# The second token tile's last products held behind the first tile's, a tail of three blocks in two streams, and a shorter log1p

## The chip, the cores and the metric

The kernel runs on one core of a Trainium2 chip. The metric is the device time of one execution in microseconds (us), the median of the runs shown. The core's engines are called PE (TensorE matmul), DVE (VectorE), ACT (ScalarE), POOL (GpSimd) and SP (SyncE, which issues the transfers).

## The reference

The program is two chained transformers of two layers each, on 256 tokens of width 1024, in fp32. Cut to what the change touches:

```python
def first_block(x, p, ...):                     # two layers
    for layer in range(2):
        hn = rmsnorm(h, gains[0])
        mix = mixer_ab(hn, ...) if layer % 2 == 0 else mixer_c(hn, ...)
        h = h + rmsnorm(mix, gains[1])
        hn = rmsnorm(h, gains[2])
        ff = square(relu(hn @ w_up[layer])) @ w_down[layer]
        h = h + rmsnorm(ff, gains[3])
        gate = sigmoid(h @ w_ple_gate[layer])
        h = h + gate * (p[layer] @ w_ple[layer])
def second_block(x, mem, ...):                  # two layers
    for l in range(2):
        h = rms_norm(x) @ w_in[l]               # columns of five attention groups
        o_a, o_b, o_c, o_d = mla(h), fox(h), moba(h), diff(h)
        o_e = memory_attention(h, rms_norm(mem) @ mem_w_kv[l])
        x = x + concat(o_a, o_b, o_c, o_d, o_e) @ w_o[l]
        xn = rms_norm(x)
        x = x + (silu(causal_conv(xn @ w_gate)) * (xn @ w_up)) @ w_down
```

`mixer_ab` (gated delta rule and mLSTM) turns its gate inputs with softplus and log-sigmoid, and fox (attention with a forget gate) does so with a log-sigmoid; both are built on log(1 + e) with e = exp(-|y|).

## The kernel before

**Tiling.** The 256 tokens are two token tiles, t = 0 and t = 1, of 128 rows. The residual `h` lies with tokens on partitions; its transposed halves `aTh` and `aTl` are the operands of the products. Each fp32 product is done as three products of split operands (`hi`/`lo` of the weight with `aTh`/`aTl` or with `w` tiles), which `nmm` (L806) writes. A product of 128 rows with 512 columns adds into a PSUM bank (`ps`).

**Streams.** `stream` (L819) runs such products over weight blocks: `seq` gives pairs (block, tile), and `nmm` is called for each. `lagged(n, lag)` lets tile 1 follow tile 0 by `lag` blocks; `tail_lagged(n, tail)` alternates the tiles, but in the last `tail` blocks writes all of tile 0's first and then tile 1's. When a tile's last block is written, `done` spawns that tile's further chain (bias, norm, transposes, next stage). Streams with one column block (one pair of banks for each tile) are the output projections `w0o`, `w1o` and `wo{l}`, the gate `wg{l}`, the memory projection `wk{l}` and the narrow `wi0{l}`; `wd{l}`, the down projection of `ff1` (L1526), is written by its own loop and has four banks in `down`.

**What sets the order.** The code issues nothing directly. `Recorder.note` (L341) records every operation with a cost (`price`, L365), its predecessors (who wrote or read its tiles before) and a lag to each engine (`LAG`, L265). `order` then lists them again: of the operations that are ready, each engine gets the one that can start first, and among those the one with the highest rank, which is the longest path of costs and lags to the end of the program. The best of seven such arrangements is issued by `issue`, so that every instruction of the profile bears the line L613 (L625 in the changed kernel), and groups are told apart by tile names. Weights come over SP's queue into 2 `raw` buffers, ACT and DVE split them into 4 `hi`/`lo` buffers, there are 32 `w2` buffers, and 8 PSUM banks.

**Where stages meet.** After `wd{l}`'s last product for a tile, `post(t)` does: a multiplication on DVE, two squares with row sums on ACT, the reciprocal root on POOL, a scaled addition into `h` on DVE, and then transposes of `h` on PE (eight of 128x128 for a tile), copies to `aTh`/`aTl`, and the products of `wg{l}`. Each other meeting of two stages has such a chain too.

Of the kernel before, what the change touches and what calls it, by code (L numbers as in the profile page):

```python
# [15 lines left out]
OP = mybir.AluOpType  # L16
# [241 lines left out]
class Recorder:  # L258
# [7 lines left out]
           "act": {"pe": 271, "act": 160, "dve": 142, "pool": 155, "sp": 1220},  # L266
           "dve": {"pe": 270, "act": 128, "dve": 127, "pool": 155, "sp": 1220},
           "pool": {"pe": 200, "act": 90, "dve": 69, "pool": 97, "sp": 1220},
           "sp": dict.fromkeys(("pe", "act", "dve", "pool", "sp"), 2050)}

    def __init__(self, nc):
        self.engines = {"pe": nc.tensor, "act": nc.scalar, "dve": nc.vector, "pool": nc.gpsimd, "sp": nc.sync}
        self.ops, self.pools, self.tile_pool, self.seen = [], {}, {}, {}
        self.run = None


    @contextmanager
    def together(self, share=1):

        self.run = []  # L280
        yield
        op = self.ops[self.run[0]]
        op.cost = op.cost / share + 200 * (share > 1)
        self.run = None

    def engine(self, name):
        rec = self
# [53 lines left out]
    def note(self, eng, call, args, kwargs):  # L341
        op = Op()
        op.eng, op.call, op.args, op.kwargs = eng, call, args, kwargs
        op.preds, op.succs, op.tiles, op.alt, op.more = {}, [], [], None, []
        op.table = self.TABLES.get(args[2], 0) if call == "activation" and args[2] != AF.Copy else None
        isap = lambda x: hasattr(x, "tensor") or hasattr(x, "tag_meta")
        outs = [kwargs[k] for k in ("out", "accum_out") if k in kwargs and isap(kwargs[k])]
        ins = [v for k, v in kwargs.items() if k not in ("out", "accum_out") and isap(v)]
        rest = [a for a in args if isap(a)]
        if "out" not in kwargs:  # L350
            outs.append(rest.pop(0))
        op.cost, op.lag = self.price(op, outs[-1], rest + ins), self.LAG[eng]
        if self.run:
            i = self.run[0]
            first = self.ops[i]
            first.more.append((call, args, kwargs))
            first.cost += op.cost
            op = first
        else:
            i = len(self.ops)  # L360
            self.ops.append(op)
            if self.run is not None:
                self.run.append(i)
        for x, write in [(x, False) for x in rest + ins] + [(x, True) for x in outs]:
            for b in self.boxes(x):  # L365
                self.touch(i, op, b, write)
# [294 lines left out]
def program(ctx, tc, A, out, dbg=None):  # L661
    nc = tc.nc
    rec = Recorder(nc)
    act, dve, pe, sp, pool = (rec.engine(n) for n in ("act", "dve", "pe", "sp", "pool"))
# [150 lines left out]
    def tail_lagged(n, tail):  # L815
        s = [(i, t) for i in range(n - tail) for t in range(2)]
        return s + [(i, t) for t in range(2) for i in range(n - tail, n)]

    def stream(name, items, acts, kpb, halves_, n, seq, done, before=None):  # L819


        first, last = {}, {}
        for t in range(2):
            for i, tt in seq:
                if tt == t:
                    first.setdefault((items[i][0], t), i)
                    last[items[i][0], t] = i
        banks, live = {}, {}
        w = halves_ * n
        for i, t in seq:  # L830
            c, b, k0 = items[i]
            if i not in live:
                live[i] = block(name, b, kpb, w)
            if before is not None:
                before(items[i], t)
            if (c, t) not in banks:
                banks[c, t] = [acc() for _ in range(halves_)]
            hi, lo = live[i]
            for j in range(kpb):
                nmm(banks[c, t], acts(t, k0 + j), hi[:, j, :], lo[:, j, :],  # L840
                    first[c, t] == i and j == 0, last[c, t] == i and j == kpb - 1, n)
                if (j + 1) * 3 * halves_ % 6 == 0:
                    loom.step()
            if last[c, t] == i:
                done(c, t, banks.pop((c, t)))

    def a_T(t, k):
# [251 lines left out]
    def mixer_ab(end):  # L1099
        nab = gain(14)  # L1100
        done = {}
        st = {}

        def gates(bank):
# [4 lines left out]
            e, u, z, ln = (w2()[:, :256] for _ in range(4))  # L1109
# [1 line left out]
            act.activation(e, e, AF.Exp)  # L1111
            dve.tensor_scalar(u, e, 1.0, None, op0=OP.add)
            act.activation(ln, u, AF.Ln)
            dve.tensor_scalar(u, u, -1.0, None, op0=OP.add)
            dve.scalar_tensor_tensor(z, u, 0.0, e, op0=OP.is_equal, op1=OP.mult)
            dve.tensor_scalar(u, u, 1e-30, None, op0=OP.max)
            dve.reciprocal(u, u)
            dve.tensor_tensor(ln, ln, e, op=OP.mult)
            dve.tensor_tensor(ln, ln, u, op=OP.mult)
            dve.tensor_tensor(ln, ln, z, op=OP.add)  # L1120
            dve.scalar_tensor_tensor(ln, y, 0.0, ln, op0=OP.max, op1=OP.add)
            ca = small(1)
            act.activation(ca, col("alog"), AF.Exp)
# [314 lines left out]
            loom.join(*([("B", j - 2)] if j >= 2 else [("A", j, t)]))  # L1438

        items = [(0, j, 2 * j) for j in (2, 3, 0, 1)]  # L1440
        stream("w0o", items, lambda t, k: done[k // 2, t](k % 2), 2, 2, 512, tail_lagged(4, 2), end, before)


    def mixer_c(r, end):
# [32 lines left out]
        def nat_done(c, t, banks):  # L1477
# [2 lines left out]
        items = [(c, 2 * c + i, 4 * i) for c in (2, 0, 1) for i in range(2)]  # L1480
        stream("w1n", items, a_T, 4, 1, 512, lagged(6, 2), nat_done)
        items = [(0, j, 2 * j) for j in range(4)]
        stream("w1o", items, lambda t, k: done[k // 2, t](k % 2), 2, 2, 512, tail_lagged(4, 2), end,
               lambda it, t: loom.join(("C", it[1], t)))


# [209 lines left out]
    def mixers2(l, r, e, mem, tab, lam, end):  # L1696
# [70 lines left out]
        def forget():  # L1767

            y, e, u, z, ln, lg = (small(8) for _ in range(6))
            for t in range(2):  # L1770
                dve.tensor_copy(y[:, 4 * t : 4 * t + 4], st["fx", t])
            dve.scalar_tensor_tensor(e, y, -1.0, y, op0=OP.mult, op1=OP.min)
            act.activation(e, e, AF.Exp)
            dve.tensor_scalar(u, e, 1.0, None, op0=OP.add)
            act.activation(ln, u, AF.Ln)
            dve.tensor_scalar(u, u, -1.0, None, op0=OP.add)
            dve.scalar_tensor_tensor(z, u, 0.0, e, op0=OP.is_equal, op1=OP.mult)
            dve.tensor_scalar(u, u, 1e-30, None, op0=OP.max)
            dve.reciprocal(u, u)
            dve.tensor_tensor(ln, ln, e, op=OP.mult)  # L1780
            dve.tensor_tensor(ln, ln, u, op=OP.mult)
            dve.tensor_tensor(ln, ln, z, op=OP.add)
            dve.scalar_tensor_tensor(lg, y, 0.0, ln, op0=OP.min, op1=OP.subtract)
            yield
            yield
            b = wk()
            pe.matmul(b[:, 0:4], cfv("triu"), lg[:, 0:4], start=True, stop=True)
            pe.matmul(b[:, 4:8], cfv("triu"), lg[:, 4:8], start=True, stop=False)
            pe.matmul(b[:, 4:8], cfv("ones"), lg[:, 0:4], start=False, stop=True)
            c = small(8)  # L1790
            dve.tensor_scalar(c, b[:, 0:8], -8.0, None, op0=OP.mult)
            st["decay"] = c
# [368 lines left out]
```

## Time and profile before

| what | value |
|---|---|
| device time, median of 3 runs | 1399.25 us (1395.28 to 1400.75) |
| the profiled execution's own time | 1395.2 us |
| its span in the trace | 1393.4 us |
| PE busy | 1359.3 us (98%) |
| DVE busy | 998.3 us (72%) |
| ACT busy | 786.4 us (56%) |
| POOL busy | 56.4 us (4%) |

The span is what lies between the first and the last instruction of the trace; the profiled execution's own time is 1.8 us longer, and 4.05 us below the median of the runs. Busy shares are averages over the whole program, whose stages have different limits. Of PE's row, ends of pipelined products are modelled, so idle time inside a dense run of products does not all show.

### The profile page before, as it was taken

To read this page: it belongs to the slowest core of one execution; us is meant where nothing else is said; L and a number is where in the kernel's file an instruction comes from. 1 tells how busy PE (TensorE), PEld (TensorE's weight loads), DVE (VectorE), ACT (ScalarE), POOL (GpSimd) and SP (SyncE) were. 2 spreads that over 40 slices of the span, in tenths; PEclk is the share of its full clock that TensorE was granted. 3 is DMA by queue.
4 is the path that set the end of the run, shared out by engine and by line. 5 is a ranking of instruction groups with operands and counts; after the bars stand their busy time and mean duration, and the time that the engine had idled before them with its cause. 6 is when DMAs were issued, how large, how long until landed. Compare 5 with 4: busy or idle time off the path is not lost.

```text
span 1393.4 us, 23108 instructions
## 1 busy us (share of the span) xinstructions
PE 1359.3 (98%) x8768; PEld 1199.4 (86%) x8774; DVE 998.3 (72%) x2417; ACT 786.4 (56%) x1800; POOL 56.4 (4%) x93
## 2 busy tenths in 40 slices
PE   6999999999999999999999999999999999999998
PEld 6899889999787799998787877999998877899997
DVE  6994876666677876566789798575767999576664
ACT  6665554444554854445576596454546679364443
POOL 0000210000010010000020000000001000000000
PEclk9999999999999999999999999999999999999999
DMA  8332354445543364445555243454545523345553
GB/s 329 134 126 99 114 212 182 182 184 194 212 147 141 139 224 179 185 182 194 207 193 206 91 142 132 152 211 153 212 155 205 187 90 99 144 153 210 182 189 114
DMA packets 36400, 236.36 MB, mean 170 GB/s; under 512 B 4160, under 2 KB 4416, under 8 KB 10176
## 3 DMA queue, kind: packets, MB, share of 16 engines
q1 hardware_dynamic: 36288, 234.88, 46.4%
q8 instruction: 69, 1.13, 0.3%
q14 instruction: 43, 0.35, 0.1%
HBM read 233.82 MB, written 1.05 MB: 169 GB/s over the span
## 4 chain that ended last, share of the span: by engine, by line
PE 88%; DVE 6%; ACT 4%; issue 1%; DMA 1%; SPq 0%; POOLq 0%; POOL 0%; ACTq 0%; DVEq 0%
PE ps L613 88%; ACT w L613 3%; DVE w L613 3%; DVE s L613 2%; DMA cf<-in_cf 1%; DVE lo L613 1%; ACT hi L613 1%; DVE h L613 0%; ACT L613 0%; SPq L613 0%; POOLq L2157 0%; DVE hi L613 0%; ACT aTh L613 0%; POOL s L613 0%; ACTq L613 0%
## 5 line engine op out<-in xcount | busy, mean ns | idle before, releaser
L613 ACT ACTIVATE hi<-raw 128x512 fp32r<-128x512 f32 (+1 forms) x793 | 437.6, 620 | 297.7 <-PE ps L613 244.9
L613 DVE TENSOR_TENSOR lo<-raw,hi 128x512 fp32r<-128x512 f32 (+1 forms) x844 | 526.0, 678 | 51.4 <-ACT hi L613 48.1
L613 PE MATMUL ps<-hi,w 128*128 128x512 f32 (+1 forms) x1272 | 379.1, 395 | 0.5 <-ACT w L613 0.5
L613 PE MATMUL ps<-aTl,hi 128*128 128x256 f32 x1256 | 316.7, 280 | 0.0
L613 PE MATMUL ps<-aTh,hi 128*128 128x256 f32 x1256 | 316.3, 281 | 0.0
L613 PE MATMUL ps<-aTh,lo 128*128 128x256 f32 x1256 | 312.5, 280 | 0.0
L613 PEld LDWEIGHTS ps<-hi,w 128*128 128x128 f32 x1272 | 225.2, 188 | 36.1 <-issue 1.9
L613 PEld LDWEIGHTS ps<-aTh,hi 128*128 128x128 f32 x1256 | 224.8, 188 | 9.4 <-ACT hi L613 0.4
L613 PEld LDWEIGHTS ps<-aTl,hi 128*128 128x128 f32 x1256 | 225.1, 188 | 8.3 <-issue 0.4
L613 PEld LDWEIGHTS ps<-aTh,lo 128*128 128x128 f32 x1256 | 223.6, 189 | 9.9 <-DVE lo L613 1.0
L613 PE MATMUL ps<-lo,w 128*128 128x512 f32 (+1 forms) x636 | 205.9, 393 | 0.0
L613 ACT ACTIVATE w<-ps 128x512 f32<-128x512 f32 (+3 forms) x261 | 128.3, 535 | 130.4 <-PE ps L613 119.9
L613 PE MATMUL ps<-hi,aTh 128*128 128x512 f32 (+2 forms) x480 | 148.4, 366 | 3.7 <-ACT w L613 2.5
L613 DVE CAST hi<-raw 128x512 fp32r<-128x512 f32 x51 | 21.8, 427 | 177.8 <-PE ps L613 177.8
L613 PE MATMUL ps<-lo,aTh 128*128 128x512 f32 (+2 forms) x480 | 147.2, 365 | 0.0
L613 PE MATMUL ps<-hi,aTl 128*128 128x512 f32 (+2 forms) x480 | 147.2, 365 | 0.0
L613 ACT ACTIVATE w<-w 128x512 fp32r<-128x512 f32 (+5 forms) x143 | 74.9, 535 | 95.3 <-DVE w L613 93.0
L613 PEld LDWEIGHTS ps<-lo,w 128*128 128x128 f32 x636 | 112.6, 188 | 17.0 <-issue 0.8
L613 PE MATMUL ps<-cf,w 128*128 128x128 f32 (+1 forms) x572 | 94.7, 279 | 17.4 <-DMA cf<-in_cf 10.6
L613 PE MATMUL ps<-w,w 128*64 128x128 f32 (+10 forms) x912 | 109.5, 299 | 0.6 <-ACT w L613 0.5
L613 PEld LDWEIGHTS ps<-w,w 128*128 128x128 f32 (+4 forms) x912 | 88.7, 171 | 20.0 <-ACT w L613 7.4
L613 PEld LDWEIGHTS ps<-hi,aTh 128*128 128x128 f32 x480 | 86.8, 190 | 16.2 <-ACT w L613 2.8
(105 smaller groups left out, 1143.8 us busy)
## 6 DMA issues: line engine op xcount, KB each, us to landing
raw<-in_wu SPq DMA_DIRECT2D x32, 1024.0 KB, 4.8
raw<-in_wd SPq DMA_DIRECT2D x32, 1024.0 KB, 5.0
raw<-in_fg SPq DMA_DIRECT2D x22, 1024.0 KB, 4.8
raw<-in_fu SPq DMA_DIRECT2D x22, 1024.0 KB, 4.8
raw<-in_fd SPq DMA_DIRECT2D x22, 1024.0 KB, 4.8
raw<-in_wi SPq DMA_DIRECT2D x20, 1024.0 KB, 4.8
raw<-in_w0t SPq DMA_DIRECT2D x10, 1024.0 KB, 5.5
raw<-in_wo SPq DMA_DIRECT2D x10, 1024.0 KB, 4.8
```

The source lines that it names most:

```text
L613: getattr(self.engines[op.eng], call)(*args, **kwargs)
```

## The change

There are four parts. A context `behind` gives every PE operation recorded in it a further predecessor. `stream` uses it in streams with one column block: once tile 0's last block is written, the last recorded operation is kept in `ended`, and all products of tile 1 that are written afterwards may start only behind it. `tail_lagged` gets 3 in place of 2 in `w0o` and `w1o`. In the table of lags SP to SP goes from 2050 to 0. And log1p is done with four operations in place of seven, in `gates` (tiles of 128x256) and `forget` (8 wide).

```diff
-           "sp": dict.fromkeys(("pe", "act", "dve", "pool", "sp"), 2050)}
+           "sp": {"pe": 2050, "act": 2050, "dve": 2050, "pool": 2050, "sp": 0}}
...
+    @contextmanager
+    def behind(self, *ops, only=None):
+        self.hold, self.only = ops, only
+        yield
+        self.hold = ()
+
+    def last(self):
+        return len(self.ops) - 1
...
             self.ops.append(op)
+            if self.hold and self.only in (None, eng):
+                op.preds.update(dict.fromkeys(self.hold, True))
...
-                nmm(banks[c, t], acts(t, k0 + j), hi[:, j, :], lo[:, j, :],
-                    first[c, t] == i and j == 0, last[c, t] == i and j == kpb - 1, n)
+                with rec.behind(*(ended if t else ()), only="pe"):
+                    nmm(banks[c, t], acts(t, k0 + j), hi[:, j, :], lo[:, j, :],
+                        first[c, t] == i and j == 0, last[c, t] == i and j == kpb - 1, n)
                 if (j + 1) * 3 * halves_ % 6 == 0:
                     loom.step()
             if last[c, t] == i:
+                if t == 0 and len(last) == 2:
+                    ended.append(rec.last())
                 done(c, t, banks.pop((c, t)))
...
             act.activation(ln, u, AF.Ln)
-            dve.tensor_scalar(u, u, -1.0, None, op0=OP.add)
-            dve.scalar_tensor_tensor(z, u, 0.0, e, op0=OP.is_equal, op1=OP.mult)
-            dve.tensor_scalar(u, u, 1e-30, None, op0=OP.max)
-            dve.reciprocal(u, u)
-            dve.tensor_tensor(ln, ln, e, op=OP.mult)
-            dve.tensor_tensor(ln, ln, u, op=OP.mult)
-            dve.tensor_tensor(ln, ln, z, op=OP.add)
+            dve.scalar_tensor_tensor(u, u, -1.0, e, op0=OP.add, op1=OP.subtract)
+            dve.tensor_scalar(z, e, 0.5, -1.0, op0=OP.mult, op1=OP.add)
+            dve.tensor_tensor(u, u, z, op=OP.mult)
+            dve.tensor_tensor(ln, ln, u, op=OP.add)
...
-        stream("w0o", items, lambda t, k: done[k // 2, t](k % 2), 2, 2, 512, tail_lagged(4, 2), end, before)
+        stream("w0o", items, lambda t, k: done[k // 2, t](k % 2), 2, 2, 512, tail_lagged(4, 3), end, before)
...
-        stream("w1o", items, lambda t, k: done[k // 2, t](k % 2), 2, 2, 512, tail_lagged(4, 2), end,
+        stream("w1o", items, lambda t, k: done[k // 2, t](k % 2), 2, 2, 512, tail_lagged(4, 3), end,
```

PE has the same products and transposes in both kernels; their order differs. Two places follow, each on PE.

**The end of `wd0` and the start of `wg0`.** Here ps_537 and ps_538 are the banks of tile 0's down projection, ps_539 and ps_540 those of tile 1; ps_735 and ps_736 take the transposes of h_81 (tile 0), ps_744 and ps_745 those of h_82 (tile 1); ps_749 and ps_750 are `wg0`'s banks of tile 0, ps_757 one of tile 1. Before:

```order
L613 MATMUL ps_539<-hi_725,w_720 128x512
L613 MATMUL ps_537<-hi_725,w_719 128x512
L613 MATMUL ps_538<-hi_725,w_719 128x512
L613 MATMUL ps_537<-lo_726,w_719 128x512
L613 MATMUL ps_537<-hi_725,w_720 128x512
L613 MATMUL ps_538<-lo_726,w_719 128x512
L613 MATMUL ps_538<-hi_725,w_720 128x512
L613 MATMUL ps_744<-cf,h_82 128x128 x4
L613 MATMUL ps_745<-cf,h_82 128x128 x4
L613 MATMUL ps_735<-cf,h_81 128x128 x4
L613 MATMUL ps_757<-hi_747,aTh 128x512
```

All four down banks end together, and the transposes of both tiles follow with nothing between them. In the changed kernel tile 0's banks end earlier:

```order
L625 MATMUL ps_538<-hi_725,w_720 128x512
L625 MATMUL ps_537<-hi_725,w_720 128x512
L625 MATMUL ps_539<-hi_711,w_697 128x512
L625 MATMUL ps_540<-hi_711,w_697 128x512
L625 MATMUL ps_539<-lo_712,w_697 128x512
L625 MATMUL ps_540<-lo_712,w_697 128x512
```

Between this and the next piece stand 27 more products of tile 1's banks; they end so:

```order
L625 MATMUL ps_540<-hi_725,w_719 128x512
L625 MATMUL ps_735<-cf,h_81 128x128 x4
L625 MATMUL ps_539<-lo_726,w_719 128x512
L625 MATMUL ps_540<-lo_726,w_719 128x512
L625 MATMUL ps_539<-hi_725,w_720 128x512
L625 MATMUL ps_540<-hi_725,w_720 128x512
L625 MATMUL ps_736<-cf,h_81 128x128 x4
L625 MATMUL ps_750<-hi_747,aTh 128x512
L625 MATMUL ps_750<-lo_748,aTh 128x512
```

After 12 more products of `wg0` for tile 0, tile 1's transposes begin, one at a time among further products of tile 0:

```order
L625 MATMUL ps_750<-lo_753,aTh 128x512
L625 MATMUL ps_749<-lo_748,aTh 128x512
L625 MATMUL ps_744<-cf,h_82 128x128
L625 MATMUL ps_750<-hi_752,aTl 128x512
L625 MATMUL ps_744<-cf,h_82 128x128
```

Tile 0's down products have moved ahead of tile 1's, and tile 1's transposes behind tile 0's gate products. The end of `wd1` and the start of `wg1` have moved in the same way; there 21 products stand between the last of `wd1` and the first transpose of tile 1.

**The end of `w0o`.** ps_476 and ps_477 are tile 0's two banks, ps_478 and ps_479 tile 1's; ps_529 and ps_533 belong to `wp0`, whose products need nothing of `w0o`; ps_500, ps_501, ps_516 and ps_517 take the transposes that follow. Before:

```order
L613 MATMUL ps_476<-lo_488,w_367 128x512
L613 MATMUL ps_476<-hi_487,w_367 128x512
L613 MATMUL ps_478<-hi_487,w_386 128x512
L613 MATMUL ps_477<-lo_488,w_367 128x512
L613 MATMUL ps_477<-hi_487,w_367 128x512
L613 MATMUL ps_478<-lo_488,w_386 128x512
L613 MATMUL ps_478<-hi_487,w_386 128x512
L613 MATMUL ps_479<-hi_487,w_386 128x512 x2
L613 MATMUL ps_479<-lo_488,w_386 128x512
L613 MATMUL ps_479<-hi_487,w_386 128x512
L613 MATMUL ps_533<-hi_527,w_524 128x512
```

Tile 0's banks end 9 and 6 products ahead of the last product of `w0o`. Eighteen products of `wp0` lie between the last of `w0o` and the first transposes (of ps_500). In the changed kernel one bank of tile 0 ends some 55 products ahead of the other banks,

```order
L625 MATMUL ps_478<-lo_475,w_438 128x512
L625 MATMUL ps_479<-lo_475,w_438 128x512
L625 MATMUL ps_476<-hi_474,w_431 128x512
L625 MATMUL ps_477<-hi_487,w_367 128x512
L625 MATMUL ps_478<-hi_474,w_438 128x512
L625 MATMUL ps_479<-hi_474,w_438 128x512
```

and the other ends with tile 1's:

```order
L625 MATMUL ps_476<-hi_487,w_367 128x512
L625 MATMUL ps_478<-hi_487,w_386 128x512
L625 MATMUL ps_476<-lo_488,w_367 128x512
L625 MATMUL ps_476<-hi_487,w_367 128x512
L625 MATMUL ps_479<-hi_487,w_386 128x512
L625 MATMUL ps_478<-lo_488,w_386 128x512
L625 MATMUL ps_478<-hi_487,w_386 128x512
L625 MATMUL ps_479<-lo_488,w_386 128x512
L625 MATMUL ps_479<-hi_487,w_386 128x512
L625 MATMUL ps_529<-hi_527,w_524 128x512
```

The predecessor that `behind` adds is the last operation of ps_477, the second bank in the order written; ps_476's products are not held to it and have moved to the end. There are 22 products of `wp0` now between the last of `w0o` and the first transposes.

## Rows read from the trace of the kernel before

**Rows 1.** The page: busy time by engine; the chain that ended last.

```profile
PE 1359.3 (98%) x8768; PEld 1199.4 (86%) x8774; DVE 998.3 (72%) x2417; ACT 786.4 (56%) x1800; POOL 56.4 (4%) x93
...
PE 88%; DVE 6%; ACT 4%; issue 1%; DMA 1%; SPq 0%; POOLq 0%; POOL 0%; ACTq 0%; DVEq 0%
```

**Rows 2.** Waits of PE over the span: for what, us in total, times, longest.

```profile
PE ps L613 <- ACT w L613: 6.6, 13, 2.5
PE ps L613 <- DVE w L613: 3.9, 3, 1.8
```

**Rows 3.** Timeline, 375 to 381 us: start, length, engine, what, [idle before <-releaser].

```profile
375.50 0.69 DVE L613 TENSOR_TENSOR w<-ps,gb 128x512 f32<-128x512 f32 x1 [1.30 <-PE ps L613]
...
378.49 0.56 POOL L613 TENSOR_TENSOR s<-s,nhalf 128x1 f32<-128x1 f32 x1 [173.68 <-DVE s L613]
...
380.01 2.73 DVE L613 SCALAR_TENSOR_TENSOR h<-w,s,h 128x512 f32<-128x512 f32 x4
...
380.86 2.79 PE L613 MATMUL ps<-cf,h 128*128 128x128 f32 x12 [3.35 <-issue]
```

**Rows 4.** Windows: us, PE PEld DVE ACT POOL busy (x), granted clock, DMA.

```profile
381.00:383.00 2.00, 2.00 (x10) 2.00 (x11) 2.00 (x4) 1.02 (x3) 0.16 (x1) 0.50 0.68 244
383.00:385.00 2.00, 2.00 (x10) 1.70 (x9) 1.62 (x4) 1.70 (x4) 0.00 (x0) 0.50 0.00 0
385.00:387.00 2.00, 2.00 (x8) 1.62 (x7) 1.58 (x4) 1.61 (x3) 0.00 (x0) 0.64 0.00 0
684.00:686.00 2.00, 2.00 (x10) 2.00 (x11) 2.00 (x4) 1.00 (x3) 0.15 (x1) 0.50 0.71 272
686.00:688.00 2.00, 2.00 (x13) 1.77 (x12) 1.58 (x4) 1.90 (x5) 0.00 (x0) 0.80 0.27 102
759.50:762.00 2.50, 2.44 (x11) 2.02 (x12) 2.50 (x20) 1.41 (x5) 0.00 (x0) 1.00 1.06 387
```

**Rows 5.** Timeline of PE alone, at five other places.

```profile
195.14 0.63 PE L613 MATMUL ps<-cf,w 128*128 128x128 f32 x4 [1.79 <-DVE w L613]
195.53 0.48 PE L613 MATMUL ps<-hi,w 128*128 128x512 f32 x1
...
409.02 0.73 PE L613 MATMUL ps<-hi,aTh 128*128 128x512 f32 x2 [0.71 <-ACT aTh L613]
...
683.89 2.79 PE L613 MATMUL ps<-cf,h 128*128 128x128 f32 x12 [3.41 <-DVE h L613]
...
759.56 0.50 PE L613 MATMUL ps<-hi,aTh 128*128 128x512 f32 x1 [2.52 <-ACT w L613]
...
1200.97 1.29 PE L613 MATMUL ps<-cf,w 128*128 128x128 f32 x8 [1.54 <-DVE w L613]
```

**Rows 6.** Timeline of PE, 857 to 862 us, end of the first second-block mixer.

```profile
857.64 1.76 PE L613 MATMUL ps<-hi,w 128*128 128x512 f32 x7
...
861.28 0.39 PE L613 MATMUL ps<-lo,w 128*128 128x512 f32 x1
```

**Rows 7.** Timeline of DVE at the same place.

```profile
863.75 1.29 DVE L613 TENSOR_TENSOR h<-ps,h 128x512 f32<-128x512 f32 x2 [0.22 <-PE ps L613]
...
867.49 1.40 DVE L613 SCALAR_TENSOR_TENSOR w<-h,s,gb 128x512 f32<-128x512 f32 x2
```

**Rows 8.** Groups of DVE by shape, 20 to 70 us: busy us, mean ns.

```profile
L613 DVE TENSOR_TENSOR w<-w,w 128x256 f32<-128x256 f32 x5 | 2.0, 405 | 0.0
L613 DVE RECIPROCAL w<-w 128x256 f32<-128x256 f32 x1 | 1.7, 1733 | 0.0
...
L613 DVE TENSOR_SCALAR w<-w 128x256 f32<-128x256 f32 x4 | 1.1, 276 | 0.0
```

**Rows 9.** Windows of 20 us in the gate stage and two attention stretches.

```profile
60.00:80.00 20.00, 19.69 (x160) 19.03 (x162) 19.88 (x47) 12.46 (x29) 0.00 (x0) 1.00 0.43 158
440.00:460.00 20.00, 19.39 (x138) 13.19 (x138) 20.00 (x79) 15.58 (x69) 0.00 (x0) 1.00 0.07 27
800.00:820.00 20.00, 19.22 (x147) 14.97 (x147) 18.16 (x61) 19.95 (x69) 0.00 (x0) 1.00 0.41 133
```

More of the change, by code (lines that the diff above doesn't have):

```diff
@@ L273, in __init__ @@
         self.ops, self.pools, self.tile_pool, self.seen = [], {}, {}, {}
-        self.run = None
+        self.run, self.hold = None, ()
     @contextmanager
@@ L827, in stream @@
                     last[items[i][0], t] = i
-        banks, live = {}, {}
+        banks, live, ended = {}, {}, []
         w = halves_ * n
@@ L1775, in forget @@
             act.activation(ln, u, AF.Ln)
[L1776 to L1782, printed above, removed]
+            dve.scalar_tensor_tensor(u, u, -1.0, e, op0=OP.add, op1=OP.subtract)
+            dve.tensor_scalar(z, e, 0.5, -1.0, op0=OP.mult, op1=OP.add)
+            dve.tensor_tensor(u, u, z, op=OP.mult)
+            dve.tensor_tensor(ln, ln, u, op=OP.add)
             dve.scalar_tensor_tensor(lg, y, 0.0, ln, op0=OP.min, op1=OP.subtract)
```

## The prediction

> **What bounds the kernel now.** I read the page first. PE is busy 98% of the span and the chain that ended last runs on PE for 88% of it [rows 1]. What PE does is the same in both kernels, so the change can only win back time in which PE stands still or runs below its clock. The idle time is small: 1393.4 - 1359.3 = 34.1 us, in which lies the first load, which no part of the change touches. Its causes come from the table of PE's waits: ACT or DVE writing a `w` tile are the releasers of 6.6 and 3.9 us, in 16 waits [rows 2]. Two waits are long by themselves: 3.35 us at 380.86, and 3.41 us at 683.89 [rows 3, 5]. Both stand where a down projection ends and `wg` begins.
>
> A wait there costs more than its length. In the windows behind the first, the granted clock is 0.50 from 381 to 385 us and 0.64 from 385 to 387; behind the second it is 0.50 from 684 to 686 and 0.80 to 688 [rows 4]. 0.50 is 1.2 GHz, the lower of TensorE's two levels (2.4 GHz is the other). At half clock, half of the time is lost: 0.50 x 4 + 0.36 x 2 = 2.7 us behind the first, 0.50 x 2 + 0.20 x 2 = 1.4 us behind the second. So the two places cost 3.35 + 2.7 = 6.1 us and 3.41 + 1.4 = 4.8 us.
>
> Other places where PE stands still: 1.79 us before the transposes behind `w0o`, 0.71 us before the first products of `w1n` behind the gate of layer 0, 2.52 us at 759.56 (products of `wi0` wait until ACT has copied a bank of the memory projection) and 1.54 us behind `wo1` [rows 5].
>
> **The hold: the two `wg` boundaries.** Tile 1's chain at 380 us shows what must be covered. Its DVE multiplication starts at 375.50, POOL's root at 378.49, the addition into `h` at 380.01, the transposes at 380.86: 5.36 us from the bank's last product [rows 3]. I take 4.4 to 5.3 us for one tile's chain when it has the engines to itself or shares them, the lower end by taking off about 1 us in which DVE and ACT worked for the other tile; that is an estimate from the same row. Before, both tiles' banks end together, and nothing lies between them and the transposes. In the changed kernel 32 products of tile 1 stand between tile 0's last and its transposes. The pace of such products: 16 from 857.64 to 861.28, 3.64 / 16 = 0.2275 us each [rows 6]. 32 make 7.3 us, more than the chain: tile 0's transposes wait for nothing. Why do they move, if the hold is only in `wg`? `wg`'s products of tile 1 now hang behind tile 0's, so that the longest path to the end leads through tile 0's down products, and the list takes them first.
>
> Tile 1 is the weak spot. From its last product to its first transpose there are 16 products and four transposes, about 3.6 + 0.4 = 4.1 us; the chain wants 4.4 to 5.3. A wait of 0.3 to 1.2 us is possible, and in layer 1, with 21 products (4.8 us), one of 0 to 0.5 us. What stands behind that wait is tile 0's gate products, which are ready.
>
> PE keeps the order it was given. The row at 195.14 shows it: four transposes wait 1.79 us for DVE, and the product of `wp0` listed next, whose operands come from elsewhere, runs at 195.53, behind them [rows 5]. The Trainium skill ("TensorE: Matmul & The Clock Gate", "Step-by-step: what each phase is for") says the same: only weight loads are pulled ahead, matmuls stay in program order. By that rule alone, which speaks against this change, a late transpose of tile 1 stops all that is ready behind it; the trace agrees with 1.79 us.
>
> So: `wg0` 6.1 less 0.4 = 5.7 us (bounds 3.3, if the clock falls all the same, and 6.1); `wg1` 4.8 less 0.1 = 4.7 us (3.4 to 4.8). The 0.71 us behind `wg0` should go too, since tile 0's gate now ends ahead of tile 1's products: 0.7 (0 to 0.7).
>
> **The hold: other streams.** (Products that I count here and that the pieces above don't show are counted in the same listing.) It hangs on one operation, the last product of the second bank, so one of tile 0's two banks is ordered ahead and the other is free to slip. At `w0o` it does: ps_476 ends with tile 1's banks. Its cover is 5 + 22 = 27 products after the change and 6 + 18 = 24 before, which is 0.7 us more for a chain that came 1.79 us late. But the other tile is in the same plight; I count 0 (0 to 0.7). At `wo1` the same pattern gives one product less of cover: -0.2 us. At `wo0` into `fg0` there is no wait before, and now there may be one. Tile 0 has 19 products to its transposes, 4.3 us, tile 1 has 13 and some transposes, about 3.5 us. The chain there, from the additions at 863.75 to the end of the scaling at 867.49 + 1.40 = 868.89, is 5.1 us as an outer bound; less the first addition and half of the last pair it is about 3.9 [rows 7]. So tile 1 lacks 0.4 to 1.6 us. In addition products of the second memory projection, which could fill such a gap, are held too. I take -0.8 (-1.6 to 0).
>
> The 2.52 us at 759.56 hang on ACT's copy of a bank [rows 5]. The memory stream and `wi0` are both held and listed anew there, so the products around the copy are others. I take +1.8 of it, between 0 (the same bank is again freed late) and 2.5, near the upper end because such a wait needs several banks full at once, and the memory stream's two tiles now end one after the other.
>
> Attention stretches: from 440 to 460 us DVE is busy 20.00 of 20 us and PE 19.39, from 800 to 820 us ACT 19.95 and PE 19.22 [rows 9]. PE is 0.6 to 0.8 us short in 20 us, and the held streams lie beside them. Over some 140 us of such stretches this is about 5 us, to win or to lose. I take 0.
>
> **Tail of three blocks.** In `w0o` and `w1o` tile 0 starts its last three blocks in a row. No product is added. The chain behind tile 1 of `w1o` then has 24 products, 5.5 us, over it. I count it at 0; the bounds are those of `w0o` above.
>
> **Shorter log1p.** Removed are two TENSOR_SCALAR, one SCALAR_TENSOR_TENSOR, one RECIPROCAL and three TENSOR_TENSOR of 128x256: 0.55 + 0.41 + 1.73 + 1.22 = 3.91 us of DVE. Added are one SCALAR_TENSOR_TENSOR, one TENSOR_SCALAR and two TENSOR_TENSOR: 0.41 + 0.28 + 0.81 = 1.50 us, the SCALAR_TENSOR_TENSOR taken like a TENSOR_TENSOR [rows 8]. DVE gets 2.4 us back in a stage where it is the busier engine (19.88 of 20 us, PE 19.69) [rows 9]. Its lead there is passed on to PE only in part, since PE waits for nothing most of the time: I take 1.2 (0 to 2.4). In `forget` the tiles are 8 wide and lie beside dense products: 0.
>
> **SP's lag.** It changes the planner's view of back-to-back transfers, not what is transferred. SP's list of 96 transfers is nearly unchanged: 0.
>
> **The sum.** 5.7 + 0.7 + 4.7 + 0 - 0.2 - 0.8 + 1.8 + 0 + 1.2 = 13.1 us. The profiled execution, 1395.2 us, would become 1382.1. It lies 4.05 us below the median of the runs, so for the median I take 1399.25 - 13.1 = 1386.1 us. Of this kernel's time, differences under 0.5% (7.0 us) can't be told from none.
>
> **Rivals.**
>
> *Tile 1's transposes stop PE as the `h` chain did.* If contention on DVE makes the chain longer than the 5.36 us seen, the wait is over 1.2 us at both boundaries. The clock fell behind idle times of 3.35 and 3.41 us and was still 1.00 behind 2.52 us [rows 4, 5]. If it fell again, each place would give back the wait and the half-clock loss. With the waits at 1.2 and 0.5 and the clock lost as before, the two give 6.1 - 1.2 - 2.7 = 2.2 and 4.8 - 0.5 - 1.4 = 2.9, in place of 10.4: 1391.4 us. Against it: between the waits PE has 32 dense products. Chance 0.15.
>
> *The held products are missed (slower than before).* Products of tile 1 in `w1o` (36), `wo0` and `wo1` (24 each) could be used as filler while tile 0's attention finishes; held, they must come after. All of it is 84 x 0.2275 = 19 us of work. If PE found nothing else in that time, the result is 1386.1 + 19 = 1405 us; it is slower than before once more than 13.1 us (58 products) go uncovered. For it: ACT and DVE are full in these stretches [rows 9], so a product less isn't made up. Against it: the list puts tile 1's `w1n` products there instead, and the same work is only moved. Chance 0.09, of which 0.06 over the bound of 0.5%; a smaller loss of this kind, about 5 us (1391), has 0.11.
>
> *The change doesn't do what it says.* The hold ties one bank, and a list by rank may fall back elsewhere what it wins at `wg`: 1399 us or a little less. Against it: at `wg0` and `wg1` the order does show tile 0 ahead. Chance 0.06.
>
> *More is won:* the attention stretches give 5 us and log1p its full 2.4: 1380 us. Chance 0.12.
>
> **How the numbers follow.** The forecast (1382 to 1391) has 0.47. Faster by over 0.5%, below 1392.3, are it, the case of more, nearly all of the small loss and half of the first rival: 0.47 + 0.12 + 0.10 + 0.07 = 0.76. Slower by over 0.5% is 0.06, within it 0.18. The range goes from 1377 (the upper bounds of all terms, 22 us) to 1396, where the lower bounds of the two `wg` places are left (3.3 + 3.4 = 6.7, less the losses at `wo0` and half of those in attention, 4.1, and none of the others: 1396.7).
>
> **What would show it.** Right: no wait over 1.5 us before the transposes that begin `wg0` and `wg1`, granted clock 1.00 in their windows; the wait in the middle of `wi0` gone or under 1 us; no RECIPROCAL of 128x256 in the gate stage; PE's idle time down by about 9 us. Wrong: a wait of 1 us or more at tile 1's transposes, a lower clock there, new waits between `wo0` and `fg0`, or PE's busy time in the attention windows lower than in the rows of before.

## Result and the profile after

The changed kernel takes 1378.93 us (median of 4 runs, 1377.46 to 1380.64), the kernel before, run beside it, 1397.84 us (median of 4 runs). The ratio is 0.9865, with a 95% interval of 0.984 to 0.9889: 18.9 us or 1.35% faster. The profiled execution of the changed kernel has a span of 1375.6 us, that of before 1393.4, so the two traces differ by 17.8 us. The forecast was 1386.1 us, in a range of 1377 to 1396: right in its direction and inside the range, with a gain of 13.1 us where 18.9 came.

The page of the changed kernel, as in [rows 1]:

```profile
PE 1352.7 (98%) x8767; PEld 1193.8 (87%) x8774; DVE 1002.0 (73%) x2421; ACT 786.7 (57%) x1796; POOL 43.3 (3%) x84
...
PE 89%; DVE 8%; ACT 2%; issue 1%; DMA 0%; POOL 0%; SPq 0%; ACTq 0%; DVEq 0%
```

PE's idle time has gone from 34.1 to 22.9 us, and 10 us of that is the first load, as before. The other 6.6 us of the 17.8 are busy time (1359.3 to 1352.7): the same products ran in less time, and of that the lost half-clock time at the two `wg` boundaries, 2.7 + 1.4 us by the prediction's reckoning, would be the larger part. The table of PE's waits (us in total, times, longest) answers to [rows 2]:

```profile
PE ps L625 <- DMA cf<-in_cf: 10.0, 1, 10.0
PE ps L625 <- DVE w L625: 4.0, 2, 2.9
PE ps L625 <- DVE aTl L625: 2.0, 4, 0.6
PE ps L625 <- ACT w L625: 1.1, 2, 0.7
```

ACT's waits went from 6.6 us in 13 times to 1.1 in 2. The waits of 3.35 and 3.41 us [rows 3, 5] are gone. One wait has become longer: 2.9 us for a `w` tile of DVE, at the end of `wo1`, where it was 1.54.

At `wg0` and `wg1` the timeline of PE alone, 374 to 381 us and 672 us, answers to [rows 3] and to the row at 683.89 in [rows 5]; the last row is the end of `wo1`, where the row at 1200.97 stood:

```profile
374.81 0.60 PE L625 MATMUL ps<-cf,h 128*128 128x128 f32 x4
...
380.30 0.27 PE L625 MATMUL ps<-cf,h 128*128 128x128 f32 x1
...
672.85 0.50 PE L625 MATMUL ps<-hi,aTl 128*128 128x512 f32 x1 [0.61 <-DVE aTl L625]
...
1183.60 1.89 PE L625 MATMUL ps<-cf,w 128*128 128x128 f32 x8 [2.94 <-DVE w L625]
```

Tile 0's transposes at 374.81 and tile 1's at 380.30 wait for nothing. At `wg1` a wait of 0.61 us is left. The windows (PE, PEld, DVE, ACT, POOL busy, then the granted clock) show what the clock did at these places, as [rows 4] did:

```profile
374.00:378.00 4.00, 4.00 (x23) 3.31 (x22) 3.39 (x6) 2.36 (x6) 0.00 (x0) 1.00 0.60 205
378.00:382.00 4.00, 4.00 (x21) 3.23 (x20) 3.93 (x8) 2.56 (x5) 0.55 (x1) 1.00 0.94 389
382.00:386.00 4.00, 4.00 (x19) 3.29 (x18) 3.88 (x7) 2.44 (x5) 0.00 (x0) 1.00 0.66 225
670.00:675.00 5.00, 4.39 (x21) 3.32 (x20) 5.00 (x10) 4.18 (x10) 1.25 (x2) 1.00 0.61 203
1183.60:1185.00 1.40, 1.40 (x7) 1.39 (x8) 1.40 (x3) 0.97 (x3) 0.87 (x2) 0.53 0.05 18
1185.00:1186.30 1.30, 1.30 (x7) 1.06 (x6) 1.30 (x3) 0.86 (x2) 0.00 (x0) 0.50 0.00 0
```

The clock stays at 1.00 through both `wg` boundaries, where it had been at 0.50. Behind the 2.94 us at the end of `wo1` it is now 0.53 and 0.50. In the kernel before, the window behind the 1.54 us there had 1.00:

```profile
1201.00:1203.00 2.00, 1.44 (x9) 1.00 (x10) 1.81 (x4) 2.00 (x6) 1.31 (x1) 1.00 0.11 37
```

To see where the 17.8 us come from, the two traces were laid over each other by work: each PE instruction counts with the median time from its start to the next start for its shape, the sum up to an instruction is its place, and the times of equal places are compared. The table gives, for stretches of before's time, what each kernel gained (minus) or lost there, in us. "again" is a second profile of the changed kernel, and shows what repeats: all stretches agree within 0.9 us but the first, where the two differ by 1.6. The other columns are the experiments below.

```
stretch, us    what lies there       changed again hold   log1p  wg    no wg  down  both
                                                   only   only   only         24    banks
  20 to  160   w0n, gates              -0.4   1.2   0.9   0.5   -0.8   -1.0   -0.7   -0.2
 160 to  220   end of w0o              -1.1  -1.0   3.0   0.1    0.7   -0.5    1.0   -0.6
 220 to  360   ff1 of layer 0           0.5   0.6   0.1  -0.2    0.2    0.7    1.1    0.3
 360 to  420   wd0, wg0, w1n           -7.0  -7.1  -5.2  -0.6   -6.0   -4.6   -4.1   -7.1
 420 to  500   attention of w1o        -2.2  -2.7  -0.8   0.1    0.5   -2.3   -0.5   -2.1
 500 to  660   ff1 of layer 1           0.8   0.9   1.5   0.4    0.5    0.7    0.3    1.1
 660 to  700   wd1, wg1                -4.1  -4.1  -4.9   1.5   -4.1   -1.0   -3.2   -5.1
 700 to  780   wi0 and after           -1.9  -2.3  -1.4  -2.1   -1.2   -2.0   -2.4   -1.6
 780 to  860   attention, layer 0      -3.4  -3.5  -3.4   0.0    0.5   -3.4   -1.2   -3.6
 860 to  880   wo0 into fg0             1.7   1.7   2.0   0.0    0.0    1.7    0.0    2.4
 880 to 1040   ff2 of layer 0          -0.1  -0.2  -0.1  -0.3   -0.3   -0.1    0.3    0.0
1040 to 1100   fd0 into layer 1         1.1   1.1   1.1   0.0    0.0    1.5    0.1    1.2
1100 to 1180   attention, layer 1      -1.8  -2.2  -1.7   0.7    0.1   -1.6   -0.8   -2.2
1180 to 1220   wo1 into fg1             1.5   0.6   0.3   0.4    0.8    2.3    1.0   -2.5
1220 to 1360   ff2 of layer 1          -0.5  -0.2  -0.6   0.6   -0.1   -0.5   -0.7    0.3
```

With 0.6 us at the first load, the changed kernel's column makes 17.5 us. The two `wg` boundaries are 11.1 of it, the attention stretches 7.4, `wi0` 1.9, the end of `w0o` 1.1; 4.3 us are given back where `wo0`, `fd0` and `wo1` end.

### The profile page after: what moved, and what is told of

It reads as the page before. It is cut to its first block, busy times and chain, and to the rows that moved or that the text cites. A ratio compares the mean times of both kernels' runs of the same rounds, so it can differ in the third digit from the quotient of the medians.

```text
span 1375.6 us, 23089 instructions
## 1 busy us (share of the span) xinstructions
PE 1352.7 (98%) x8767; PEld 1193.8 (87%) x8774; DVE 1002.0 (73%) x2421; ACT 786.7 (57%) x1796; POOL 43.3 (3%) x84
## 4 chain that ended last, share of the span: by engine, by line
PE 89%; DVE 8%; ACT 2%; issue 1%; DMA 0%; POOL 0%; SPq 0%; ACTq 0%; DVEq 0%
PE ps L625 89%; DVE w L625 3%; DVE lo L625 3%; DVE s L625 2%; ACT w L625 1%; ACT L625 0%; DVE aTl L625 0%; DMA h<-in_x 0%; ACT hi L625 0%; DVE h L625 0%; POOL s L625 0%; DVE hi L625 0%; DVE tab L625 0%; ACT s L625 0%; ACT aTh L625 0%
## 5 line engine op out<-in xcount | busy, mean ns | idle before, releaser
L625 ACT ACTIVATE hi<-raw 128x512 fp32r<-128x512 f32 (+2 forms) x788 | 432.5, 619 | 285.6 <-PE ps L625 236.5
L625 PE MATMUL ps<-aTh,hi 128*128 128x256 f32 x1256 | 333.2, 280 | 0.7 <-DVE aTl L625 0.6
L625 PE MATMUL ps<-aTl,hi 128*128 128x256 f32 x1256 | 330.9, 280 | 0.8 <-DVE aTl L625 0.8
L625 PE MATMUL ps<-aTh,lo 128*128 128x256 f32 x1256 | 331.1, 280 | 0.5 <-DVE lo L625 0.5
L625 PE MATMUL ps<-lo,w 128*128 128x512 f32 x636 | 216.8, 395 | 0.0
L625 ACT ACTIVATE w<-ps 128x512 f32<-128x512 f32 (+2 forms) x261 | 126.4, 517 | 125.7 <-PE ps L625 118.2
L625 PE MATMUL ps<-hi,aTh 128*128 128x512 f32 (+2 forms) x480 | 160.4, 372 | 0.0
L625 PE MATMUL ps<-lo,aTh 128*128 128x512 f32 (+2 forms) x480 | 158.2, 367 | 0.1
L625 ACT ACTIVATE w<-w 128x512 f32<-128x512 f32 (+5 forms) x144 | 75.7, 534 | 107.6 <-DVE w L625 105.1
L625 PEld LDWEIGHTS ps<-cf,w 128*128 128x128 f32 (+1 forms) x572 | 72.6, 144 | 30.2 <-DVE w L625 12.6
```

Of the source, the lines that this page charges most:

```text
L625: getattr(self.engines[op.eng], call)(*args, **kwargs)
```

## The experiments

Each was timed beside the kernel before, in five rounds, and the ratio is to that kernel. The experiments ran in several such sets; across sets, ratios are compared.

**The hold alone.** The changed kernel without the rest:

```diff
-           "sp": {"pe": 2050, "act": 2050, "dve": 2050, "pool": 2050, "sp": 0}}
+           "sp": dict.fromkeys(("pe", "act", "dve", "pool", "sp"), 2050)}
...
-        stream("w0o", items, lambda t, k: done[k // 2, t](k % 2), 2, 2, 512, tail_lagged(4, 3), end, before)
+        stream("w0o", items, lambda t, k: done[k // 2, t](k % 2), 2, 2, 512, tail_lagged(4, 2), end, before)
...
-        stream("w1o", items, lambda t, k: done[k // 2, t](k % 2), 2, 2, 512, tail_lagged(4, 3), end,
+        stream("w1o", items, lambda t, k: done[k // 2, t](k % 2), 2, 2, 512, tail_lagged(4, 2), end,
...
+            (the seven operations of the old log1p in place of the four)
```

> The kernel before with the hold alone: no tail of three blocks, the old log1p, the old lag of SP. If the hold makes the whole gain (my theory), the ratio to before is 0.986 to 0.989, with no wait over 1 us at the start of wg0 and wg1. If the shorter log1p carries the 1.2 us that I counted for it or more, or the tail some us, it stands 2 to 4 us above the changed kernel, at a ratio of 0.988 to 0.990.

1386.01 us, ratio 0.9912 (0.9898 to 0.9926): about 7 us behind the changed kernel (6.6 by ratio), more than either theory allowed. The table says where: 4.1 us at the end of `w0o`, 1.8 at `wg0`, 1.4 in the attention behind `w1o`. The timeline of PE at the end of `w0o`:

```profile
191.33 0.73 PE L625 MATMUL ps<-hi,w 128*128 128x512 f32 x2 [0.66 <-ACT hi L625]
...
195.86 1.26 PE L625 MATMUL ps<-cf,w 128*128 128x128 f32 x8 [1.70 <-DVE w L625]
197.72 0.44 PE L625 MATMUL ps<-cf,w 128*128 128x128 f32 x2 [0.60 <-DVE w L625]
...
198.93 0.66 PE L625 MATMUL ps<-cf,w 128*128 128x128 f32 x4 [0.42 <-DVE aTl L625]
```

and the same place in the changed kernel:

```profile
193.07 0.60 PE L625 MATMUL ps<-cf,w 128*128 128x128 f32 x4
...
196.39 0.36 PE L625 MATMUL ps<-aTh,hi 128*128 128x256 f32 x1 [0.56 <-DVE aTl L625]
```

Four waits stand where the kernel before had one of 1.79 us and the changed kernel has one of 0.56: 0.66 us for a split weight, then 1.70, 0.60 and 0.42 us before transposes. In the list of the hold alone only 10 products of `wp0` are left between the last of `w0o` and the first transposes, where there were 18 before and are 22 in the changed kernel. So the hold by itself harms the end of `w0o`. That the tail mends it is shown by the two kernels with one tail each, below.

**The shorter log1p alone.** The kernel before with only the four operations in place of the seven (`gates` and `forget`).

> The kernel before with the shorter log1p alone. By my sum 1.2 us are won (between 0 and 2.4), all of it between 40 and 140 us. The rival reads the trace of the changed kernel, where PE's work up to 140 us is done only 0.2 us earlier once the start of the first load is taken off: then the ratio is 1.000 within the measurement, and DVE alone is shorter in that stage.

1396.72 us, ratio 0.9982 (0.9971 to 0.9994). By the medians that is 0.8 us and by the ratio 2.5 (0.8 to 4.1), so the size doesn't tell the two expectations apart, and the place is neither's: the table has +0.5 us in the gate stage, less than the 1.6 us by which two profiles of one kernel differ there, and -2.1 us at `wi0`, some 700 us later, where the wait of 2.52 us [rows 5] is gone. The column as a whole doesn't show a gain: it has +1.5 us at `wd1` and `wg1`, and this trace's span is 1395.0 us, 1.6 longer than that of before. The timeline of ACT in the kernel before shows what made that wait (`w<-ps,mr` is the copy that frees a bank of the memory projection):

```profile
755.87 0.69 ACT L613 ACTIVATE w<-ps,mr 128x512 f32<-128x512 f32 x1 [0.98 <-issue]
756.45 0.62 ACT L613 ACTIVATE hi<-raw 128x512 fp32r<-128x512 f32 x1
756.98 0.40 ACT L613 ACTIVATE w<-w 128x256 f32<-128x256 f32 x1
757.28 1.65 ACT L613 ACTIVATE hi<-raw 128x512 fp32r<-128x512 f32 x3
758.84 0.67 ACT L613 ACTIVATE w<-ps,mr 128x512 f32<-128x512 f32 x1
```

Between the two copies ACT splits weights (`hi<-raw`, three of them in 1.65 us). In the kernel with the shorter log1p the same timeline has the two copies together:

```profile
758.33 1.27 ACT L625 ACTIVATE w<-ps,mr 128x512 f32<-128x512 f32 x2 [1.79 <-issue]
759.48 0.63 ACT L625 ACTIVATE hi<-raw 128x512 fp32r<-128x512 f32 x1
```

A change of seven small operations at 50 us let the list put ACT's work at 757 us in another order. That is the one clear gain in its trace; whether it makes up the gain of the ratio is not shown.

**The hold in `wg0` and `wg1` alone**, on the kernel before:

```diff
-                if t == 0 and len(last) == 2:
+                if t == 0 and len(last) == 2 and name.startswith("wg"):
```

> The kernel before with the hold in wg0 and wg1 alone. If the two boundaries are separate from the rest (my sum: 5.7 + 0.7 + 4.7 = 11.1 us), the ratio is 0.992, the waits of 3.35 and 3.41 us are gone, and the wait of 2.52 us in wi0, the one of 1.79 us behind w0o and the gaps in the attention stretches stay. If the gain comes from the list as a whole, which any hold shakes up, these other places change too and the ratio can be anything from 0.985 to 0.998.

1387.09 us, ratio 0.9915 (0.9901 to 0.9928). -6.0 and -4.1 us at the two boundaries, as the changed kernel within 1.1. The attention stretches and the ends of `w0o`, `wo0` and `wo1` stay within 0.8 us of before, as the first theory has it; the single wait of 2.52 us in `wi0` is gone, which it has not.

**The changed kernel without the hold in `wg0` and `wg1`:**

```diff
-                if t == 0 and len(last) == 2:
+                if t == 0 and len(last) == 2 and not name.startswith("wg"):
```

> The changed kernel without the hold in wg0 and wg1, all else left. By the step of my prediction that tile 0's down products move because wg's products of tile 1 hang behind tile 0's, both waits come back with their low clock: 11 us above the changed kernel, a ratio to before of 0.994. By the rival, that a hold in any later stream raises the rank of tile 0's path up to there, tile 0's down products still end 24 products (5.5 us) ahead, the waits stay away, and the ratio stays at 0.986 to 0.989.

1383.42 us, ratio 0.9892 (0.9879 to 0.9906): between the two expectations, at the edge of the rival's. At `wg0` 4.6 of 7.0 us stay, at `wg1` 1.0 of 4.1. The order of the list has tile 0's down products ahead in both places, with 24 (`wd0`) and 27 (`wd1`) of tile 1's between them and the transposes. What is lost at `wg1` is behind the transposes, in the timeline of PE:

```profile
674.00 1.04 PE L625 MATMUL ps<-cf,h 128*128 128x128 f32 x8
675.84 0.51 PE L625 MATMUL ps<-hi,aTh 128*128 128x512 f32 x1 [0.81 <-ACT aTh L625]
...
678.15 0.79 PE L625 MATMUL ps<-hi,aTl 128*128 128x512 f32 x1 [1.10 <-DVE aTl L625]
```

Tile 0's eight transposes come behind all of tile 1's down products here, and nothing is left to fill the time in which ACT and DVE copy them: the first products of `wg1` wait 0.81 and 1.10 us for `aTh` and `aTl`. The windows there (as above):

```profile
676.60:678.20 1.60, 0.50 (x3) 0.06 (x2) 1.60 (x5) 1.50 (x4) 0.55 (x1) 1.00 1.01 425
678.20:680.00 1.80, 1.80 (x4) 1.43 (x5) 1.80 (x4) 0.69 (x2) 0.00 (x0) 0.50 0.92 348
680.00:681.30 1.30, 1.30 (x5) 0.99 (x4) 1.30 (x3) 0.47 (x1) 0.00 (x0) 0.50 0.05 16
```

The clock is at 0.50 for 3 us behind these two.

**Only the down products ordered.** No hold in any stream; in `ff1`'s last loop the last 24 products of tile 1 go behind tile 0's last two (`behind` as in the change; `stop0` starts empty):

```diff
-                nmm(down[t], (hid[0][:, j, ts(t)], hid[1][:, j, ts(t)]), w[0][:, j, :], w[1][:, j, :],
-                    u == 0 and j == 0, u == n - 1 and j == 1)
+                with rec.behind(*(stop0 if t else ()), only="pe"):
+                    nmm(down[t], (hid[0][:, j, ts(t)], hid[1][:, j, ts(t)]), w[0][:, j, :], w[1][:, j, :],
+                        u == 0 and j == 0, u == n - 1 and j == 1)
+                if t == 0 and u == n - 1 and j == 1:
+                    stop0.extend((rec.last() - 1, rec.last()))
```

> The kernel before, no hold in any stream, old log1p, old tails: only the last 24 down products of tile 1 in wd0 and wd1 are held behind tile 0's last one. In the list 19 to 20 products (4.5 us) then stand between tile 0's last and its transposes. If the order of the down products is the whole cause at the two wg boundaries, most of their 10.9 us goes: ratio 0.992 to 0.994, waits there under 1 us. If the gain there needs wg's own products in order too, tile 1's transposes come ahead of tile 0's gate products and stop PE again: ratio 0.996 or more.

1387.32 us, ratio 0.9929 (0.9914 to 0.9944). -4.1 and -3.2 us at the two places, without any hold in `wg`. What is left there are short waits before the transposes of either tile, 0.59 and 0.57 us at `wg0`, and behind `wg0` a wait of 1.17 us for `aTh`, at the place where before had 0.71 and the changed kernel has none. In the timeline of PE:

```profile
378.88 0.63 PE L625 MATMUL ps<-cf,h 128*128 128x128 f32 x4 [0.59 <-issue]
...
385.37 0.66 PE L625 MATMUL ps<-cf,h 128*128 128x128 f32 x4 [0.57 <-DVE h L625]
...
407.10 0.72 PE L625 MATMUL ps<-hi,aTh 128*128 128x512 f32 x2 [1.17 <-ACT aTh L625]
```

These three make 2.3 of the 2.9 us by which the changed kernel is ahead in this stretch: the hold in `wg` is worth something of its own there. The first wait stands behind 18 products of cover. The second is the one of the first rival: tile 1's transposes, late, in front of products of tile 0. The Trainium skill ("TensorE: Matmul & The Clock Gate", "Step-by-step: what each phase is for") has matmuls stay in program order, and the trace agrees: PE stands still for 0.57 us.

**The same with 6 products held** (`if t and u == n - 1 and j == 1`):

> The same with only the last 6 down products of tile 1 held, which leaves 17 products (3.9 us) of cover. If the cover against the chain of 4.4 to 5.4 us decides, a wait of 0.5 to 1.5 us is back before the transposes of tile 0 at each boundary, and the run is 1 to 3 us slower than the one with 24; if a wait of that size lowers the granted clock again, 3 to 6 us slower.

1392.44 us, ratio 0.9964 (0.9952 to 0.9977), 5.1 us behind the kernel with 24, but not for the reason expected. The start of tile 0's chain (DVE's multiplication) and PE's wait at the two boundaries, and last the wait in `wi0`, from the timelines:

```profile
375.30 1.37 DVE L625 TENSOR_TENSOR w<-ps,gb 128x512 f32<-128x512 f32 x2 [0.56 <-PE ps L625]
...
379.73 1.33 PE L625 MATMUL ps<-cf,h 128*128 128x128 f32 x8 [0.17 <-PE ps L625]
...
675.86 1.37 DVE L625 TENSOR_TENSOR w<-ps,gb 128x512 f32<-128x512 f32 x2 [0.53 <-PE ps L625]
...
680.34 1.29 PE L625 MATMUL ps<-cf,h 128*128 128x128 f32 x8 [0.21 <-DVE h L625]
...
755.45 0.50 PE L625 MATMUL ps<-hi,aTh 128*128 128x512 f32 x1 [2.52 <-ACT w L625]
```

PE waits 0.17 and 0.21 us, and the gain there is no smaller than with 24 (-5.1 and -3.8 us). In its list 16 products stand between, one fewer than the expectation has. Counted as the prediction counts it, from DVE's first multiplication to the first transpose, the chain took 4.4 and 4.5 us here (375.30 to 379.73, 675.86 to 680.34). In the kernel with 24 it took 4.9 us at both places, and there the transposes waited 0.59 and 0.64 us. So the kernel with the smaller hold has the shorter chain, and with it the shorter waits; why its chain is shorter is not shown. What this kernel lacks lies elsewhere: its loss between 500 and 660 us is 2.7 us (0.3 with 24), and at `wi0` the wait of 2.52 us is back.

**The changed kernel with the old log1p.**

> The changed kernel with the old log1p. By my sum it is 1.2 us slower than the changed kernel (ratio to before 0.9875, between 0.9865 and 0.988); by the rival, that the shorter log1p gives PE nothing, 0.9865 as the changed kernel. Against the kernel with the hold alone it shows the tail of three blocks, whose worth I had put at 0: if the tail only matters together with the hold, it stands 5 to 8 us below the ratio of 0.9912, and the long wait behind w0o (2.9 us in all in the kernel with the hold alone) is gone.

1379.52 us, ratio 0.9872 (0.9854 to 0.989): no difference from the changed kernel that the intervals can tell. Against the hold alone, from which it differs by the tails (and by SP's lag), it is 0.0040 lower: 5.6 us.

**The tail of three blocks in one stream alone**, all else as in the changed kernel; first in `w0o`:

```diff
-        stream("w1o", items, lambda t, k: done[k // 2, t](k % 2), 2, 2, 512, tail_lagged(4, 3), end,
+        stream("w1o", items, lambda t, k: done[k // 2, t](k % 2), 2, 2, 512, tail_lagged(4, 2), end,
```

> The changed kernel with the tail of three blocks in w0o alone (w1o has two again). The hold alone lost 4 us between 180 and 200 us against the changed kernel, where w0o ends, and about 2 us between 440 and 480 us, where w1o's attention lies. If each tail works at its own stream, this kernel keeps the gain at 195 us and loses the 2 us at 440: ratio 0.988 to 0.989. If the two places hang on one list as a whole, both change or neither.

1381.95 us, ratio 0.9893 (0.9873 to 0.9913). Over the same stretches as in the table it has -1.0 us at the end of `w0o`, as the changed kernel, and -0.6 in the attention of `w1o` in place of -2.2. Then in `w1o`, with `tail_lagged(4, 2)` in `w0o`:

> The changed kernel with the tail of three blocks in w1o alone. By the same theory the long waits behind w0o come back (4 us between 180 and 200 us) and the stretch at 440 is as in the changed kernel: ratio 0.989 to 0.990.

1384.16 us, ratio 0.9906 (0.9888 to 0.9923): +4.2 us at the end of `w0o`, -2.1 in the attention of `w1o`. Each tail works at its own stream, by the places of the gains. By ratio, taking away `w1o`'s costs about 3.8 us and taking away `w0o`'s about 5.6, while both together cost 5.6; each of these is known to some 2 us only.

The tail alone and SP's lag alone, without the hold, weren't timed: each by itself leaves every engine's list of instructions exactly as it was. SP's lag together with the hold was not taken apart from the tails.

**The hold on both banks.** `behind` gets the last product of each of tile 0's two banks:

```diff
+                if t == 0 and len(last) == 2 and last[c, t] == i and j == kpb - 1:
+                    ended.extend(range(rec.last() - halves_ + 1, rec.last() + 1))
                 if (j + 1) * 3 * halves_ % 6 == 0:
                     loom.step()
             if last[c, t] == i:
-                if t == 0 and len(last) == 2:
-                    ended.append(rec.last())
```

> The changed kernel with the hold on the last product of both of tile 0's banks, not of the second alone. If the waits that are left where mixers end (0.6 us behind w0o, 2.94 us with a granted clock of 0.50 behind it at the end of wo1) come from the bank that isn't held, they go: 5 to 6 us under the changed kernel, a ratio to before of 0.982 to 0.983. If tile 1's chain, or products that are then missing as filler in the attention stretches, take their place, it stays at 0.986 to 0.988, and a wait of another kind stands there.

1376.68 us, ratio 0.9858 (0.9844 to 0.9873). The 2.94 us at the end of `wo1` are gone. The timeline of PE at that place:

```profile
1183.01 0.39 PE L625 MATMUL ps<-hi,w 128*128 128x512 f32 x1
1183.24 1.03 PE L625 MATMUL ps<-cf,w 128*128 128x128 f32 x8
1184.52 0.39 PE L625 MATMUL ps<-hi,aTh 128*128 128x256 f32 x1 [0.25 <-ACT aTh L625]
...
1185.85 0.38 PE L625 MATMUL ps<-hi,aTl 128*128 128x256 f32 x1 [0.58 <-DVE aTl L625]
```

The transposes at 1183.24 follow the products at once, and 0.58 us is the longest wait. That is 4.0 us at this place, from +1.5 to -2.5. The run as a whole has less, so it was run again beside the changed kernel:

> The changed kernel once more, on the same chip and beside the same runs of before as the next kernel: ratio 0.985 to 0.988.

> The hold on both of tile 0's banks once more. If the 2.8 us by which its trace is ahead of the changed kernel's behind 1200 us are real, its ratio is 0.002 below that of the changed kernel beside it; if its losses of 1 to 2 us before 800 us are as real as its gain at the end of wo1, the two agree within 0.001.

1378.62 us and 0.9867 (0.985 to 0.9884) for the changed kernel, 1378.42 us and 0.9865 (0.9849 to 0.9881) for the hold on both banks. The two can't be told apart: what is won at `wo1` is lost in pieces, 0.7 us more at `wo0` among them, and the rest under what two profiles of one kernel differ by.

## Why the prediction was right, and where its sizes were off

**Order of the down products: right.** That alone gave 4.1 and 3.2 of the 7.0 and 4.1 us. Both waits went, with the half-clock time behind them: 7.0 + 4.1 = 11.1 us against 6.4 + 4.7 = 11.1 in the sum. That the two sums are equal to a tenth is luck, since each place was off by 0.6 us. Why tile 0 goes first was half told. The hold in `wg` does it alone, but the later holds together do it too: without the one in `wg`, the list still put tile 0 first. That a longer path behind tile 0 raises what comes before it is argued from how the list ranks, not shown. The chain was taken at 4.4 to 5.3 us; where it could be read it took 4.4 to 4.9.

**Tile 1's transposes (the first rival): real, but small.** They did stop PE, for 0.57 us, where only the down products were ordered. In the changed kernel they waited for nothing.

**Other streams: the terms that failed in size.** The attention stretches were put at 0, between -5 and +5. They gave 2.2 us (behind `w1o`) and 3.4 + 1.8 = 5.2 us (second block), 7.4 in all: over the upper bound, and the main reason why 18.9 us came and not 13.1. The second rival, that the held products are missed there, had the wrong sign. The kernel with the hold in `wg` alone has none of it, and the changed kernel without that hold has all of it, so the hold in the other streams is enough for it; which of `wk`, `wi0` and `wo` does it was not tried singly. Not all of it need come from a hold: with the down products ordered and no hold in any stream, 1.2 + 0.8 of the 5.2 us came too. Of the 2.2 us behind `w1o`, 1.6 hang on that stream's tail. The end of `w0o` gave 1.1 us where 0 (0 to 0.7) was counted. Part is given back at `wo0` (1.7 us, 0.8 in the sum) and `wo1` (1.5 by one profile and 0.6 by the other, 0.2 in the sum), as the argument on the bank that isn't held had it for `wo1`: held on both banks, that wait is gone. The 1.1 us at the end of `fd0` were not seen coming.

**Tail of three blocks: failed.** It was counted at 0, since it adds no product. With the hold, the two tails (and SP's lag) are worth about 5.6 us by ratio. The traces place them: 5.3 us at `w0o` (4.2 without its tail against -1.1) and 1.6 in the attention of `w1o`, taken away one at a time. Without it the hold leaves too few products over the chain of `w0o`. I had priced the two edits one by one and added them.

**`wi0`: right size, wrong reason.** 1.9 us came where 1.8 were counted. But the wait went in kernels without any hold in the memory stream, and came back in one that holds 6 down products. It hangs on whether ACT's weight copies fall between its two copies of banks.

**log1p: not seen in PE's time.** No RECIPROCAL of 128x256 is left in the gate stage. The rows of DVE by shape, 20 to 70 us (count, busy us, mean ns), answer to [rows 8]:

```profile
L625 DVE SCALAR_TENSOR_TENSOR w<-w,w 128x256 f32<-128x256 f32 x4 | 1.6, 410 | 0.0
L625 DVE TENSOR_TENSOR w<-w,w 128x256 f32<-128x256 f32 x4 | 1.6, 410 | 0.0
...
L625 DVE TENSOR_SCALAR w<-w 128x256 f32<-128x256 f32 x3 | 0.8, 281 | 0.0
```

Of the 2.4 us that DVE saves, PE's share can't be seen: -0.4 us in one profile of the changed kernel, +1.2 in the other, and 0.0005 to 0.0007 of ratio (0.7 to 1.0 us) with wide intervals. No trace shows the 1.2 us of the sum in the gate stage, and the times can't exclude them.

## What to carry to other kernels

Where two halves of a stage end together, order the whole of one ahead of the other: the second half's products cover the first half's chain, and the wait and the half-clock time behind it go together (11 us here for two places). Price edits to a list's order together, not singly: the tail changes no list alone, and with the hold it was worth about 5.6 us. Lay two traces over each other by equal work before crediting a gain to an edit; the one clear gain in the trace of the shorter log1p, 2.1 us, lay 700 us behind it.

## What the runs showed of the hardware

The granted clock doesn't follow the longest single wait alone. It fell to 0.50 behind two waits of 0.81 and 1.10 us with four products between them, and behind 2.94, 3.35 and 3.41 us, yet it was 1.00 behind a wait of 2.52 us [rows 4]. The first rival had compared single waits only; in these runs their lengths don't tell whether the clock falls.
